# The second layer's feed-forward tiles 8 to 21, computed by seven products over both token chunks at once instead of over the two halves of each chunk

## The chip, the cores and the metric

The kernel runs on one core of one Trainium2 chip. The core has five engines that run their own instruction lists and meet by semaphores: TensorE (PE, matrix products; PEld is its weight load), VectorE (DVE), ScalarE (ACT), GpSimd (POOL) and SyncE (SP), which here only starts DMAs. The metric is the device time of one execution in microseconds, as the median of three runs.

## The reference, cut to what matters

A trunk of two residual layers works on 1024 tokens of 1024 channels, everything in float32. Layer 0 mixes tokens by a Conformer convolution, layer 1 by pooling over trailing windows; each layer then has a SwiGLU feed-forward part, and a norm ends the trunk.

```
for i in range(2):
    h = modulate(rms_norm(x, norm_mix_g[i]), sh_m, sc_m)
    y = conformer_conv(h, ...) if i == 0 else multiscale_pool(h, pool_w, pool_ls)
    x = x + (1 + g_m) * y
    h = modulate(rms_norm(x, norm_ffn_g[i]), sh_f, sc_f)
    y = (silu(h @ w_gate[i]) * (h @ w_up[i])) @ w_down[i]      # 1024 -> 2816 -> 1024
    x = x + (1 + g_f) * y
return rms_norm(x, final_g)
```

The change is in the feed-forward part of layer 1: its two products with `w_gate` and `w_up`, and what stands around them.

## The kernel before

**Tiling.** Channels lie on the 128 partitions, tokens along the free axis. The tokens are cut into two chunks of 512, A and B. `x[chunk][k]` is channel tile k (of 8) of a chunk and stays in SBUF. The hidden width 2816 is 22 tiles of 128, called tiles 0 to 21 below.

**Precision.** A float32 product is made of three fast ones: each operand is split into a high part `hi` (rounded to the fast type) and a low part `lo` (what the rounding left), and hi·hi, hi·lo and lo·hi are summed in PSUM. ACT makes `hi` by a copy, DVE makes `lo` by a subtraction. For many weights the `lo` is made without DVE: ACT writes minus `hi`, and a DMA started by POOL adds the weight from DRAM onto it.

**A plain tile** (`ffn_p1`) is 48 products of 512 columns: 8 input tiles × 3 for gate, the same for up. `ffn_p2` gives a tile pair's share of the down product: for each of the 8 output tiles d, six products and then one update of `x` by DVE (`update`, the rows `x<-dn,gains,x`). I call such a group of six a slot.

**Seven products instead of eight.** Most tiles run in pairs of hidden tiles (`Pair`, `ffn_pair`). The weight of a pair is seen as 2×2 blocks (two hidden tiles × two halves of the input channels), the input as 2×2 blocks (two halves of the channels × the two halves of 256 tokens in a chunk), and Winograd's form of Strassen's scheme gives the four result blocks by seven block products. A block product (`quad`) is 4 input tiles × 3 = 12 products of 256 columns. The scheme needs four sums of input blocks, made once for a chunk (`combined`: the tiles `thi`, `tlo`), and four sums of weight blocks, made for each pair and each chunk (`Pair.prepare`: `shi`, `slo`, `w`). A pair is two units (gate, then up), each of 84 products of 256 columns. Between its block products stand up to four slots of the down product of the pair before (`Downs.slot`).

**Order of work in layer 1, before.** Chunk A: tiles 0 and 1 plain, 2 to 17 in pairs, 18 to 21 plain, with the pooling mixer of B among the last; then B: tiles 0 and 1 plain, 2 to 21 in pairs, and `ending`, which makes the last down product in two halves of 256 columns and the final norm. `pooled` starts a chunk's mixer, then takes its output product (`pool_out`, the rows `y`), then the norm ahead of the feed-forward part (`norm`, the tiles `hhi`, `hlo`).

**What sets the order.** PE's list is the order in which the code is written. DVE, ACT, POOL and SP lists are set by a scheduler when the program is built, by priorities and its own estimate of when a thing is ready; every engine then takes its own list strictly in order. Background work is written as generators (`Task`), which `pace` and `finish` advance; `finish` and `need` write all that is left of a task at that place.

**Buffers that matter.** PSUM has eight banks: six named `mm` (`bank`) and two named `ca` (`spare_bank`). `output(name, True)` takes three from the six, then one from the two, so slots of the down product go round all eight. Weight tiles `w` have 9 buffers, raw weights `raw` 4, per-chunk tiles for `hhi`/`hlo` 16 each.

Of the kernel before, what the change touches and what calls it, by code (L numbers as in the profile page):

```python
# [16 lines left out]
P = 128  # L17
D = 1024
# [101 lines left out]
def trunk(ctx, tc, xT, c, vec, ada, adan, w1, w2, wgu, wdn, wpl, wph, out):  # L120
# [46 lines left out]
    raws = ctx.enter_context(tc.tile_pool(name="raws", bufs=RAW_BUFS))  # L167
    tmp = ctx.enter_context(tc.tile_pool(name="tmp", bufs=2))
    ps = ctx.enter_context(tc.tile_pool(name="ps", bufs=BANKS, space=bass.MemoryType.PSUM))

    uid = [0]

# [76 lines left out]
    def slot(ch, name, dt=F32R):  # L249

        return slots.tile([P, ch.n], dt, tag=f"s{ch.i}", name=nm(name))
# [37 lines left out]
        return t[:, :n]  # L289


    cact = cst.tile([P, D], F32, name="cact")
# [237 lines left out]
    def sum_sq(srcs, n, into=None):  # L530
        acc = None
        for s in srcs:
            if acc is None:
                acc = temp(n, "acc", 2) if into is None else into[:, :n]
                S_.activation(acc, s, AF.Square)
            else:
                sq = temp(n)
                S_.activation(sq, s, AF.Square)
                V_.tensor_tensor(acc, acc, sq, op=ADD)
            yield  # L540
        return acc
# [27 lines left out]
        if lows is not None:  # L569
            lows.append(V_.last.ins.name)  # L570

    def norm(ch, l, ffn, key, keep=False, squares=None, **kw):
# [7 lines left out]
        for k in range(KT):  # L580
            modulated(ch, l, ffn, h, rstd, k, lows if kw else None)
            yield

# [14 lines left out]
    def own(unit_):  # L598
        return unit_[0], tuple(Own(w) for w in unit_[1])
# [465 lines left out]
    FRONT, BACK = slice(0, QUAD), slice(QUAD, D)  # L1065
    f32 = lambda t: t.bitcast(F32)

    def combined(ch):

        other = chunks[1 - ch.i]  # L1070
        h = st["h", ch.i]
        got = st["T", ch.i] = []
        for k in range(KT // 2):
            whole = []
            for hi, lo in (h[k], h[k + KT // 2]):
                t = window(ch.n, "hf")
                V_.tensor_tensor(t, f32(hi), f32(lo), op=ADD)
                whole.append(t)
            a, b = whole
            q12, q34 = temp(ch.n, "tf"), temp(ch.n, "tf")  # L1080
            V_.tensor_tensor(q12[:, LEFT], a[:, LEFT], a[:, RIGHT], op=SUB)
            V_.scalar_tensor_tensor(q12[:, RIGHT], q12[:, LEFT], -1.0, b[:, RIGHT], op0=MUL, op1=SUB)
            V_.tensor_tensor(q34[:, LEFT], b[:, RIGHT], a[:, RIGHT], op=SUB)
            V_.scalar_tensor_tensor(q34[:, RIGHT], q12[:, RIGHT], -1.0, b[:, LEFT], op0=MUL, op1=SUB)
            if k == KT // 2 - 2:
                st["rows", ch.i] = V_.last.ins.name
            yield
            row = []
            for q in (q12, q34):
                hi, lo = slot(other, "thi"), slot(other, "tlo")  # L1090
# [208 lines left out]
    def ffn_mixed(ch, l, plain, until, at_end=False, beside=None):  # L1299
# [26 lines left out]
        if until == NF:  # L1326
# [4 lines left out]
        if not at_end:  # L1331
            for i in (4, -1):
                rest[i] = own(rest[i])
        return before, paired, rest

    def ending(ch, l, fs):

# [59 lines left out]
        return emit, tuple(wdn[l, f] for f in fs)  # L1397

    def final(ch):
        acc = yield from sum_sq(x[ch.i], ch.n, cact)  # L1400
# [266 lines left out]
        need(("T", ch.i))  # L1667
        add(us)

    before, pairs, rest = ffn_mixed(B, 0, PLAIN[0], UNTIL[0])  # L1670
    put(("T", 1), lambda: combined(B))
    add(before[:2])
    put(("stats", 0), lambda: pool_stats(A))
# [71 lines left out]
```

## Time and profile before

| | |
|---|---|
| three runs | 1793.75, 1795.19 and 1796.05 us; median 1795.19 |
| the profiled execution | span 1797.1 us from the first to the last instruction |
| PE busy | 1770.1 us, 98% of the span |
| DVE busy | 1402.7 us, 78% |
| ACT busy | 1042.8 us, 58% |
| POOL busy | 556.3 us, 31% |
| DMA | 321.85 MB, mean 179 GB/s |

The profile was taken on one execution of its own; only its span is known, and it is 1.9 us longer than the median of the runs. A stretch of the span is named by its start and end in us from the first instruction. An engine's instructions overlap a little, so the time from one start to the next is shorter than the duration of one. The lists of before and of the changed kernel are the same on PE up to the first paired block of chunk A in layer 1, which stands at 1093.6 us of the profiled span.

### The profile page before, as it was taken

Reading aid. Unit: us, or ns where it says so; the run is one execution under the profiler, and the core shown is the slowest. Engines: PE = TensorE matmul, PEld = TensorE weight load, DVE = VectorE, ACT = ScalarE, POOL = GpSimd, SP = SyncE. Lnnn points to the kernel's source line nnn. Section 1 sums busy time; section 2 is a strip of 40 time slices with the busy share of each in tenths; the row PEclk is TensorE's granted clock in tenths of the full one; section 3 lists DMA queues with packets and bytes.
Section 4 is the critical chain, followed back from the end, with each engine's and each line's share of the span. In section 5 each row is a group of like instructions: output and inputs, shape, how many; then the busy total and the mean of one; then the engine's idle time right before and its main releaser. Section 6 shows DMA issues by size and latency. Waiting matters only on the chain.

```text
span 1797.1 us, 27345 instructions
## 1 busy us (share of the span) xinstructions
PE 1770.1 (98%) x10178; PEld 1537.1 (86%) x10178; DVE 1402.7 (78%) x2270; ACT 1042.8 (58%) x1682; POOL 556.3 (31%) x604
## 2 busy tenths in 40 slices
PE   9999999999999999999999999999999999999997
PEld 7777777888888888899999889999998889999997
DVE  8688946898775328989996999878769998887865
ACT  4766665877646455555556356655554566555553
POOL 0388822987734121211113611101115111011112
PEclk9999999999999999999999999999999999999999
DMA  9968766897988988877765566455555765655442
GB/s 306 284 177 249 184 154 175 216 239 205 235 206 207 236 218 196 227 205 203 205 197 138 140 171 153 130 137 141 136 130 140 170 154 140 183 141 137 128 113 59
DMA packets 112921, 321.85 MB, mean 179 GB/s; under 512 B 11026, under 2 KB 21394, under 8 KB 112787
## 3 DMA queue, kind: packets, MB, share of 16 engines
q1 hardware_dynamic: 77936, 222.56, 37.5%
q0 software_dynamic: 33696, 96.48, 30.3%
q8 instruction: 80, 1.31, 0.3%
q10 hardware_dynamic: 1154, 1.05, 0.2%
q14 instruction: 55, 0.44, 0.1%
HBM read 315.85 MB, written 4.19 MB: 178 GB/s over the span
## 4 chain that ended last, share of the span: by engine, by line
PE 90%; DVE 3%; issue 2%; ACT 2%; DMA 2%; POOL 1%; ACTq 0%; DVEq 0%; SPq 0%; POOLq 0%
PE dn L137 25%; PE up L137 24%; PE gate L137 24%; PE y L137 5%; PE a L137 3%; PE g L137 2%; PE first L137 2%; ACT w L114 1%; PE ada L137 1%; DVE t L114 1%; DVE hlo L114 1%; DMA adaw<-in_adan_dram 1%; PE var L137 1%; PE rstd L137 1%; DMA w<-in_wgu_dram 1%
## 5 line engine op out<-in xcount | busy, mean ns | idle before, releaser
L137 PE MATMUL dn<-ghi,w 128*128 128x512 f32 (+1 forms) x1440 | 474.1, 387 | 0.6 <-ACT t L114 0.6
L114 ACT CAST w<-raw 128x512 fp32r<-128x512 f32 (+1 forms) x410 | 320.5, 784 | 169.6 <-PE up L137 73.5
L114 DVE SCALAR_TENSOR_TENSOR x<-dn,gains,x 128x512 f32<-128x512 f32 (+1 forms) x360 | 262.6, 736 | 66.4 <-PE dn L137 57.5
L137 PEld LDWEIGHTS dn<-ghi,w 128*128 128x128 f32 x1440 | 269.3, 189 | 50.7 <-ACT t L114 1.0
L114 ACT ACTIVATE w<-raw 128x1024 fp32r<-128x1024 f32 (+1 forms) x234 | 204.8, 875 | 165.5 <-PE dn L137 43.7
L1161 POOL DMA_DIRECT2D w<-in_wgu_dram x100 | 87.1, 873 | 633.9 <-PE up L137 203.2
L137 PE MATMUL dn<-glo,w 128*128 128x512 f32 (+1 forms) x720 | 279.3, 388 | 0.1
L137 PE MATMUL gate<-hhi,w 128*128 128x512 f32 (+1 forms) x1008 | 275.3, 348 | 0.9 <-ACT hhi L114 0.6
L137 PE MATMUL up<-hhi,w 128*128 128x512 f32 (+1 forms) x1008 | 275.0, 347 | 0.0
L114 POOL TENSOR_TENSOR pa<-pa,pr 128x512 f32<-128x512 f32 x176 | 251.3, 1565 | 18.3 <-ACT pr L114 15.5
L137 PEld LDWEIGHTS gate<-hhi,w 128*128 128x128 f32 x1008 | 179.7, 189 | 26.7 <-ACT hhi L114 0.7
L137 PEld LDWEIGHTS up<-hhi,w 128*128 128x128 f32 x1008 | 179.9, 189 | 24.5
L137 PE MATMUL gate<-hlo,w 128*128 128x512 f32 (+1 forms) x504 | 175.4, 348 | 1.5 <-DVE hlo L114 1.5
L137 PE MATMUL up<-hlo,w 128*128 128x512 f32 (+1 forms) x504 | 175.0, 347 | 0.0
L114 DVE SCALAR_TENSOR_TENSOR ca<-u,vecs,ca 128x512 f32<-128x512 f32 x244 | 170.6, 749 | 1.0
L114 DVE TENSOR_TENSOR w<-raw,w 128x512 fp32r<-128x512 f32 (+1 forms) x176 | 137.8, 789 | 32.1 <-ACT w L114 27.7
L137 PEld LDWEIGHTS dn<-glo,w 128*128 128x128 f32 x720 | 136.1, 189 | 20.4 <-POOL glo L114 0.6
L445 POOL DMA_DIRECT2D w<-in_wgu_dram x70 | 63.1, 906 | 244.8 <-ACT w L114 222.1
L114 ACT ACTIVATE pr<-u,vecs 128x512 f32<-128x512 f32 x176 | 119.9, 718 | 27.5 <-POOL pa L114 19.7
L114 ACT CAST shi<-ny 128x512 fp32r<-128x512 f32 x100 | 62.1, 621 | 119.9 <-PE gate L137 59.5
L114 DVE TENSOR_TENSOR t<-t,up 128x256 f32<-128x256 f32 (+1 forms) x86 | 52.3, 609 | 89.2 <-PE up L137 88.3
L137 PEld LDWEIGHTS gate<-hlo,w 128*128 128x128 f32 x504 | 95.3, 189 | 15.4 <-DVE hlo L114 2.6
(203 smaller groups left out, 3751.3 us busy)
## 6 DMA issues: line engine op xcount, KB each, us to landing
raw<-in_wgu_dram SPq DMA_DIRECT2D x176, 512.0 KB, 4.8
raw<-in_wdn_dram SPq DMA_DIRECT2D x88, 512.0 KB, 5.3
w<-in_wgu_dram POOLq DMA_DIRECT2D x70, 512.0 KB, 8.0
adaw<-in_ada_dram SPq DMA_DIRECT2D x64, 512.0 KB, 5.3
w<-in_wgu_dram POOLq DMA_DIRECT2D x100, 256.0 KB, 5.7
raw<-in_w_dram SPq DMA_DIRECT2D x42, 512.0 KB, 6.7
adaw<-in_adan_dram SPq DMA_DIRECT2D x32, 512.0 KB, 5.7
w<-in_w_dram POOLq DMA_DIRECT2D x32, 512.0 KB, 8.1
```

What stands on the lines that cost most here:

```text
L114: self.last = self.order(getattr(self.eng, name)(out, *args, **kw))
L137: last_mm[0] = nc.tensor.matmul(out, lhsT, rhs, start=start, stop=stop, **kw).ins.name
L445: order(nc.gpsimd.dma_start(as_src(lo), src, accum_op=ADD))
L1161: order(nc.gpsimd.dma_start(lo, src, accum_op=ADD))
```

## The change

The gate and up products of tiles 8 to 21 take the seven-product scheme over both chunks together: the two column blocks of the input are now chunk A and chunk B, 512 columns each, instead of the two halves of one chunk. A unit (`joint_unit`) is 84 products of 512 columns and serves both chunks; the weight sums are made once for both.

- Chunk A's tiles 0 to 7 run plain. Chunk B's pooling mixer and its norm run among them, so that both chunks' inputs are there before tile 8.
- The sums of input blocks are made by `joint_rows` after B's norm: for each of four steps k, five wide sums and their splits. The sums are named t1, t2, t3 and t4. There is not room for all: t1 and t4 and the first half of B's own input (`front`) are written to DRAM (`keep`), and t1 and t4 are read back in every unit into the same eight SBUF tiles (`streamed`), t4 after the product with t1, t1 after the product with t4.
- The low parts of the weight blocks are all made by DVE (`Joint.halves`) in place of the adding DMAs.
- The down products (`JointDowns`) have a slot for each output tile and each chunk, and take their banks from `spare_bank`. They stand at fixed places within the units (`GATE_SLOTS`, `UP_SLOTS`); the first unit takes all eight slots of A's tiles 6 and 7 in one piece, the second has none.
- After the joint units B alone takes its tiles 0 and 1 plain and 2 to 7 in pairs of 256 columns; sixteen slots of the last joint pair stand between tiles 0 and 1. The ending is as before, on tiles 6 and 7.

```diff
-PLAIN = (4, 2, 2)
-UNTIL = (18, 18, 22)
+PLAIN, UNTIL = 4, 18
+WHOLE = 8
+GATE_SLOTS = (6, 9, 12, 14, 17, 19, 22, 24)
+UP_SLOTS = (3, 6, 9, 11, 14, 17, 20, 23)
...
+    class JointDowns(Downs):
+        def __init__(self, l, fs, dps, chs):
+            super().__init__(None, l, fs, dps)
+            self.todo = [(d, ch) for d in self.todo for ch in chs]
+        def slot(self, out=None):
+            d, ch = self.todo.pop(0)
+            self.load(d // 2)
+            wt = self.tiles[d // 2]
+            b = (out or spare_bank)("dn")
...
+            update(ch, d, b, gate_f, self.l)
...
+    def joint_rows():
...
+        def split(q, tiles):
+            S_.copy(tiles[0], q)
+            V_.tensor_tensor(tiles[1], q, f32(tiles[0]), op=SUB)
+            return tiles
+        def keep(name, k, tiles):
+            for dst, t in zip(st["kept", name][k], tiles):
+                sync.dma_start(dst, f32(t))
+        def whole(h, t):
+            V_.tensor_tensor(t, f32(h[0]), f32(h[1]), op=ADD)
+            return t
+        for k in range(half):
+            keep("front", k, hb[k])
+            a, c, d = whole(ha[k], ...), whole(hb[k], ...), whole(hb[k + half], ...)
+            V_.tensor_tensor(a, a, c, op=SUB)
+            V_.tensor_tensor(c, d, c, op=SUB)
+            V_.scalar_tensor_tensor(d, a, -1.0, d, op0=MUL, op1=SUB)
+            st["t2"].append(split(d, ...))
+            b = whole(ha[k + half], temp(512))
+            V_.scalar_tensor_tensor(b, d, -1.0, b, op0=MUL, op1=SUB)
+            st["t1"].append(split(a, [slot(B, n) for n in ("t1hi", "t1lo")]))
+            keep("t1", k, st["t1"][k])
+            st["t3"].append(split(c, ...))
+            keep("t4", k, split(b, [tmp.tile([P, TMPW], F32R, tag="acc", name=nm("t4"), bufs=2) for _ in range(2)]))
...
+    def joint_unit(l, me, following, downs, later, first=False, last=False):
...
+            block(a, "w11", ha[:half], True)
+            S_.copy(ra, a)
+            block(left, "w12", ha[half:], True)
+            V_.tensor_tensor(ra, ra, left, op=ADD)
+            if first:
+                for each in downs:
+                    while each.todo:
+                        each.slot(lambda n: output(n, True))
+                finish(T["rows"])
+            block(a, "s2", st["t2"], False)
+            S_.copy(rb, a)
+            block(right, "s1", st.pop("t1"), True)
+            S_.copy(qb, right)
+            t4 = streamed("t4", B)
...
+            block(a, "s3", st["t3"], False)
+            V_.tensor_tensor(qb, qb, a, op=ADD)
+            block(right, "s4", hb[half:], False)
+            V_.tensor_tensor(rb, rb, right, op=ADD)
+            block(a, "w22", t4, False)
...
+                st["t1"] = streamed("t1", B)
...
-    before, pairs, rest_a = ffn_mixed(A, 1, PLAIN[1], UNTIL[1], False, (("stats", 1), lambda: pool_stats(B, cact)))
-    add(before[:1])
-    put_eager(("T", 0), lambda: combined(A))
-    add(rest[-1:] + before[1:])
-    paired(A, pairs)
-    need(("stats", 1))
-    pooled(rest_a[:-1], B, OUT_AT)
-    before, pairs, rest = ffn_mixed(B, 1, PLAIN[2], UNTIL[2], True, ("final_a", lambda: final(A)))
+    us, joint_pend = [], rest[-1]
+    for f in range(0, WHOLE, 2):
+        us += [ffn_p1(A, 1, f, True), joint_pend, ffn_p1(A, 1, f + 1, True)]
+        joint_pend = ffn_p2(A, 1, [f, f + 1], True)
...
+    need(("nf", 1))
+    put_eager("rows", joint_rows)
+    joint, last = ffn_joint(1, WHOLE)
+    add(joint)
+    before, pairs, rest = ffn_mixed(B, 1, 2, WHOLE, True, ("final_a", lambda: final(A)))
     add(before[:1])
-    put_eager(("T", 1), lambda: combined(B))
-    add(rest_a[-1:] + before[1:])
+    put_eager(("T", 1), lambda: combined(B, (A, A, B, B)))
+    add(last)
+    add(before[1:])
     paired(B, pairs)
     add(rest)
```

The built programs show where this puts instructions. The first place is DVE's list just ahead of the first unit's products with sums of input blocks. Before, for chunk A's first pair (`tlo` is the low part of a sum of input blocks, `slo` that of a sum of weight blocks, `acc` and `ny` are sums of weight blocks):

```order
L114 SCALAR_TENSOR_TENSOR x_7_92<-dn_10223,gains,x_7_92 128x512
L114 TENSOR_TENSOR w_10411<-raw_10330,w_10411 128x512
L114 TENSOR_TENSOR ny_10363<-ny_10351,raw_10241 128x512
L114 TENSOR_TENSOR slo_10354<-ny_10351,shi_10353 128x512
L114 TENSOR_TENSOR acc_10422<-raw_10332 128x512
L114 TENSOR_TENSOR slo_10360<-acc_10357,shi_10359 128x512
L114 SCALAR_TENSOR_TENSOR tf_10286<-tf_10285,hf_10283 128x256
L114 TENSOR_TENSOR tlo_10304<-tf_10285,thi_10303 128x512
```

Now, the rows of the last two of four steps of `joint_rows` (`ha`, `hb` are sums of a chunk's high and low parts; `t2lo_11501` and `t2lo_11535` are the low parts of t2 for steps k = 2 and 3):

```order
L117 TENSOR_TENSOR t2lo_11501<-hb_11495,t2hi_11500 128x512
L117 TENSOR_TENSOR t_2225_11518<-t_11504,t_2224_11517 128x512
L117 TENSOR_TENSOR ha_11525<-ha_11525,hb_11527 128x512
L117 TENSOR_TENSOR hb_11529<-hhi_10997,hlo_10998 128x512
L117 TENSOR_TENSOR hb_11527<-hb_11529,hb_11527 128x512
L117 TENSOR_TENSOR t1lo_11542<-ha_11525,t1hi_11541 128x512
L117 SCALAR_TENSOR_TENSOR hb_11529<-ha_11525,hb_11529 128x512
L117 TENSOR_TENSOR t3lo_11548<-hb_11527,t3hi_11547 128x512
L117 SCALAR_TENSOR_TENSOR t_11538<-hb_11529,t_11538 128x512
L117 TENSOR_TENSOR t2lo_11535<-hb_11529,t2hi_11534 128x512
```

Where four sums of input blocks of a chunk stood among the weight work, five sums of 512 columns for both chunks and their low parts now stand in a row, twelve rows of DVE for each k; in DVE's list the last low part of t2 is the 74th row from the update `x_7` after the slots of A's tiles 4 and 5 on, that update counted (21 SCALAR_TENSOR_TENSOR and 53 TENSOR_TENSOR, all of 512 columns).

The second place is DVE's list beside the slots that stand alone ahead of B's pairs. Before, in the like place ahead of A's pairs, between the updates for the first slots:

```order
L114 SCALAR_TENSOR_TENSOR x_0_85<-dn_10149,gains,x_0_85 128x512
L114 SCALAR_TENSOR_TENSOR tf_10235<-tf_10235,hf_10233 128x256
L114 TENSOR_TENSOR tf_10236<-hf_10233,hf_10231 128x256
L114 TENSOR_TENSOR tlo_10212<-tf_10170,thi_10211 128x512
L114 SCALAR_TENSOR_TENSOR x_1_86<-dn_10157,gains,x_1_86 128x512
L114 TENSOR_TENSOR glo_10111<-t_10112,ghi_10110 128x512
L114 SCALAR_TENSOR_TENSOR tf_10236<-tf_10235,hf_10233 128x256
L114 TENSOR_TENSOR w_10334<-raw_10241,w_10334 128x512
L114 SCALAR_TENSOR_TENSOR x_2_87<-dn_10175,gains,x_2_87 128x512
```

Now, from the update for the second of the sixteen slots to that for the third:

```order
L117 SCALAR_TENSOR_TENSOR x_0_87<-dn_14880,gains,x_0_87 128x512
L117 SCALAR_TENSOR_TENSOR tf_14990<-tf_14990,hf_14988 128x256
L117 TENSOR_TENSOR tf_14991<-hf_14988,hf_14986 128x256
L117 TENSOR_TENSOR glo_14841<-t_14842,ghi_14840 128x512
L117 TENSOR_TENSOR tf_15064<-hf_15060 128x256
L117 SCALAR_TENSOR_TENSOR tf_14991<-tf_14990,hf_14988 128x256
L117 TENSOR_TENSOR w_15125<-raw_14847,w_15125 128x512
L117 TENSOR_TENSOR acc_15136<-raw_14849 128x512
L117 TENSOR_TENSOR acc_15148<-raw_14847,raw_14849 128x512
L117 TENSOR_TENSOR hf_15062<-hhi_10997,hlo_10998 128x512
L117 TENSOR_TENSOR tlo_15029<-tf_14990,thi_15028 128x512
L117 SCALAR_TENSOR_TENSOR x_1_80<-dn_14888,gains,x_1_80 128x512
```

Ten rows stand there between two updates, and the slots have two banks instead of eight. From the first to the last of the sixteen updates are 44 rows: 16 updates, 21 others of 512 columns and 7 of 256. The third place is SP's list within a joint unit. Before, the paired stage had weight loads alone:

```order
L1182 DMA raw_10696<-in_wdn_dram 128x2x512
L1108 DMA raw_10802<-in_wgu_dram 128x1024
L1108 DMA raw_10804<-in_wgu_dram 128x1024
L1182 DMA raw_10891<-in_wdn_dram 128x2x512
L1108 DMA raw_10982<-in_wgu_dram 128x1024
```

Now loads of t4 stand around a weight load (`t_2141` and its neighbours are t4 in DRAM):

```order
L1189 DMA raw_12124<-in_wdn_dram 128x2x512
L150 DMA t_2376_12221<-t_2141_11260 128x512
L150 DMA t_2377_12222<-t_2142_11261 128x512
L150 DMA t_2378_12225<-t_2143_11262 128x512
L150 DMA t_2379_12226<-t_2144_11263 128x512
L1115 DMA raw_12266<-in_wgu_dram 128x1024
L150 DMA t_2380_12229<-t_2145_11264 128x512
L150 DMA t_2381_12230<-t_2146_11265 128x512
```

A unit's two weights, its share of the down weights, eight tiles of t4 and eight of t1 now go through that one list, each behind the one above it.

More of the change, by code (lines that the diff above doesn't have):

```diff
@@ L579, in norm @@
         lows = []
-        for k in range(KT):
+        for k in ks:
             modulated(ch, l, ffn, h, rstd, k, lows if kw else None)
@@ new lines, in trunk @@
+    class JointDowns(Downs):
[7 more added lines that the diff above has]
+            b = (out or spare_bank)("dn")
+            for i, f in enumerate(self.fs):
+                g = st["g", ch.i, f]
+                for j, (wp, a) in enumerate(((0, 0), (0, 1), (1, 0))):
+                    matmul(b, wt[:, wp, i, (d % 2) * P : (d % 2 + 1) * P], g[a], start=i + j == 0, stop=i == 1 and j == 2)
+            update(ch, d, b, gate_f, self.l)
+            if d % 2 == 0:
+                self.load(d // 2 + 1)
+            pace()
@@ new lines, in ffn_joint, with begin @@
+    def ffn_joint(l, start):
+        mates = [Joint(l, f, which) for f in range(start, NF, 2) for which in range(2)]
+        mine = [[JointDowns(l, (start - 2, start - 1), dps, (A,)) for dps in ((0, 1), (2, 3))], []]
+        for f in range(start, NF, 2):
+            mine += [[JointDowns(l, (f, f + 1), dps, (A, B))] for dps in ((0, 1), (2, 3))]
+        def begin(take):
+            mates[0].front()
+            for each in mine[0]:
+                for dp in each.dps:
+                    each.load(dp)
+        us = [(begin, ())]
+        for i, me in enumerate(mates):
+            later = mine[i + 1]
+            us.append(joint_unit(l, me, mates[i + 1] if i + 1 < len(mates) else None, mine[i], later[0] if later else None,
+                                 i == 0, i + 1 == len(mates)))
+        return us, [alone(d) for d in (mine[-2][0], mine[-1][0])]
@@ L1668, in paired @@
         add(us)
-    before, pairs, rest = ffn_mixed(B, 0, PLAIN[0], UNTIL[0])
+    before, pairs, rest = ffn_mixed(B, 0, PLAIN, UNTIL)
     put(("T", 1), lambda: combined(B))
```

160 lines of the change are left out of this document (150 added, 10 removed).

## The prediction

> **What bounds the kernel now.** I read the page from the top: busy time, then the chain that ended last, then windows over layer 1's paired stage.
>
> ```profile
> span 1797.1 us, 27345 instructions
> PE 1770.1 (98%) x10178; PEld 1537.1 (86%) x10178; DVE 1402.7 (78%) x2270; ACT 1042.8 (58%) x1682; POOL 556.3 (31%) x604
> PE 90%; DVE 3%; issue 2%; ACT 2%; DMA 2%; POOL 1%; ACTq 0%; DVEq 0%; SPq 0%; POOLq 0%
> core 0: us, PE busy (x) PEld busy (x) DVE busy (x) ACT busy (x) POOL busy (x), PEclk, DMA share, GB/s
> 1100.00:1340.00 240.00, 240.00 (x1674) 224.27 (x1673) 187.85 (x309) 134.84 (x256) 27.23 (x38) 1.00 0.55 142
> 1400.00:1456.00 56.00, 55.32 (x252) 45.40 (x251) 51.18 (x96) 30.74 (x48) 7.82 (x9) 1.00 0.66 152
> 1460.00:1760.00 300.00, 299.59 (x2097) 279.99 (x2096) 239.29 (x392) 166.55 (x321) 32.81 (x38) 1.00 0.54 140
> ```
>
> Within A's pairs (1100 to 1340) PE is busy in every microsecond at full clock (PEclk 1.00), and B's pairs are nearly the same. There, time falls only if PE has fewer or cheaper products, and rises by every wait that is new on PE. The start of B's pairs (1400 to 1456) leaves PE idle for 0.68 us. So the sum has two kinds of terms: what the columns cost, and new waits in PE's list.
>
> **The change part by part. Products.** The chain in order of time shows whole blocks of gate products (start, length, count):
>
> ```profile
> 1003.44 5.44 PE gate L137 x24
> 1119.35 2.86 PE gate L137 x24
> ```
>
> 24 products of 512 columns take 5.44 us, 226.7 ns each; 24 of 256 columns take 2.86 us, 119 ns each. Two of the small cost 238 ns, 11 more than one of the large. PE's list loses 2520 products of 256 columns (4200 become 1680) and gains 1272 of 512; the down products are the same in number. −2520 × 0.1190 = −299.9 us and +1272 × 0.2267 = +288.4 us: **−11.5 us**.
>
> The Trainium skill ("TensorE: Matmul & The Clock Gate", section "Back-to-back issue gap") gives an isolated product N/2.4 + 2.5 ns, 109.2 for 256 columns and 215.8 for 512. By that the exchange would gain 0.7 us and the sum would be 10.8 us higher; the rows differ from it for both sizes, by more for the small one, and they decide.
>
> **The wait for the rows of the joint input.** In the first joint unit PE's list has, after the slots of A's tiles 4 and 5: tile 7's 48 products (10.9 us by the row above), two blocks of 12 (5.4), the eight slots of tiles 6 and 7 (48 products, 10.9), and then the product with t2, of which nine products (2.0) can go before the fourth k is needed. That is 29.2 us of work. On DVE, 74 rows stand from the update `x_7` after the slots of tiles 4 and 5 to t2's fourth low part. Their pace is read where DVE works without a pause:
>
> ```profile
> 1446.81 0.69 DVE L114 TENSOR_TENSOR ny<-acc,raw 128x512 f32<-128x512 f32 x1
> 1447.40 0.69 DVE L114 TENSOR_TENSOR slo<-acc,shi 128x512 fp32r<-128x512 f32 x1
> 1448.01 0.75 DVE L114 SCALAR_TENSOR_TENSOR x<-dn,gains,x 128x512 f32<-128x512 f32 x1
> 1448.67 0.42 DVE L114 TENSOR_TENSOR tf<-hf,hf 128x256 f32<-128x256 f32 x1
> 1449.00 0.42 DVE L114 SCALAR_TENSOR_TENSOR tf<-tf,hf 128x256 f32<-128x256 f32 x1
> ```
>
> From start to start a TENSOR_TENSOR of 512 columns takes 0.59 to 0.61 (I use 0.60), a SCALAR_TENSOR_TENSOR 0.66, and rows of 256 columns 0.33 and 0.34. So 21 × 0.66 + 53 × 0.60 = 45.7 us after `x_7` begins, which cannot begin before PE has made slot 7. The difference, 16.5 us, is idle time on PE even if DVE arrives on time. It does not: from B's norm (`rstd`) on, DVE has 22 rows (19 SCALAR_TENSOR_TENSOR, 3 others) ahead of `x_7`, behind an ACT copy:
>
> ```profile
> L114 ACT COPY ny<-rstd 128x512 f32<-128x512 f32 x4 | 2.3, 580 | 18.3 <-PE rstd L137 18.3
> ```
>
> 0.58 + 19 × 0.66 + 3 × 0.60 = 14.9 us, while PE goes through the eight slots of tiles 4 and 5 in 10.9: DVE is 4.0 us late. **+20.5 us** (16.5 if DVE arrives on time; 24 if an ACT copy that DVE's subtraction needs comes late in some of the steps). Behind these rows on DVE stand the updates of tiles 6 and 7's slots; they only hold PSUM banks, eight of them for eight slots, so they add nothing of their own.
>
> **The clock after that wait.** PE stands for over 15 us. The nearest row is the first norm, where PE waits for DVE too:
>
> ```profile
> 72.00:78.00 6.00, 4.55 (x24) 3.58 (x23) 4.03 (x9) 6.00 (x9) 3.27 (x3) 0.98 1.05 257
> 78.00:84.00 6.00, 6.00 (x25) 5.00 (x24) 1.68 (x10) 4.49 (x7) 6.00 (x7) 0.74 1.06 270
> ```
>
> After 1.45 us of missing work the granted clock over the next 6 us is 0.74: 6 × 0.26 = 1.6 us lost. **+1.6** (0 to 3.2, if it happens at both new waits). The skill's clock gate (the same page, "Part 1: The HAM clock gate") says that an idle window sends PE to half rate and that about 3.4 us of work bring it back, an estimate of 1.7 us for one long wait; the 0.74 agrees.
>
> **The sixteen slots that stand alone.** They follow each other on PE with nothing between them, from two banks, so slot n waits for the update of slot n−2. DVE has 16 updates, 21 other rows of 512 columns and 7 of 256 in that stretch: 16 × 0.66 + 21 × 0.60 + 7 × 0.335 = 25.5 us against 16 × 1.36 = 21.8 of products. That DVE lags there is seen in before's like place, hidden by eight banks:
>
> ```profile
> 1434.62 10.88 PE dn L137 x48
> 1436.69 0.75 DVE L114 SCALAR_TENSOR_TENSOR x<-dn,gains,x 128x512 f32<-128x512 f32 x1
> 1449.34 0.75 DVE L114 SCALAR_TENSOR_TENSOR x<-dn,gains,x 128x512 f32<-128x512 f32 x1
> ```
>
> Eight slots took PE 10.88 us; their first and last updates start 12.65 us apart. With two banks PE follows this pace: the stretch takes at least 1.5 us (to the first update) + 25.5 = 27.0, +5.2, and DVE's list arrives about 3 us late, since rows on a gate weight of the next plain tile, whose buffer PE frees only there, stand among the updates. **+8** (5, on time, to 11, twice as late).
>
> **t1, t4 and weights from DRAM.** Eight tiles of 256 KB each replace t1 by t4 and back, 2.1 MB a time. The rates seen:
>
> ```profile
> 20.00:60.00 40.00, 40.00 (x179) 33.11 (x178) 35.97 (x51) 19.81 (x31) 0.00 (x0) 1.00 0.97 327
> raw<-in_wgu_dram SPq DMA_DIRECT2D x176, 512.0 KB, 4.8
> x<-in_xT_dram SPq DMA_DIRECT2D x16, 256.0 KB, 5.9
> ```
>
> At 327 GB/s 2.1 MB take 6.4 us, the last tile about 6.4 + 3 after the first is freed (a 512 KB load alone lands in 4.8, of which 1.6 is its bytes). Between the first freed tile of t1 and the first use of t4 PE has eleven steps of three products, 11 × 0.68 = 7.5 us, and the last use is three steps (2.0) later: 9.4 against 9.5 in the units without slots, and five slots more (14.3 us) in the others. PE's list hides it, barely in the first two units. **+1** (0 to +8, a late tile in both bare units and small ones elsewhere). The low parts that DVE now makes in place of POOL's adding DMAs lie under PE: a pair of units has 34.8 us of DVE rows at the pace above against 59.8 us of PE (168 + 96 products of 226.7 ns). Without that cover each would cost its 0.60 us. The writes of t1, t4 and front go into the stretch of the first wait, whose length DVE sets.
>
> **What goes.** The waits at the old paired starts, 0.68 us at B's by the 1400 row and little at A's: **−1** (0 to −2); B's pairs still start once.
>
> **Sum** against the profiled span: 1797.1 − 11.5 + 20.5 + 1.6 + 8 + 1 − 1 = 1815.7. The profiled execution's span is 1.9 us over the median of the runs, so **1814 us** by that measure, +1.0%. The low bounds give −11.5 + 16.5 + 0 + 5 + 0 − 2 = +8.0 (1803), the high ones −11.5 + 24 + 3.2 + 11 + 8 + 0 = +34.7 (1830).
>
> **Rivals.** *DVE is no obstacle (faster).* If rows of joint_rows, which read and write SBUF alone, ran twice as fast at 512 columns as I price them, 45.7 us would be about 24 (0.33 × 74), under the 29.2 us of cover, and the alone slots would be paced by PE: 1795 − 11.5 − 1 + 1 = 1783. It decides from 0.39 us a row down. Against it: `ny<-acc,raw` and `slo<-acc,shi` above are such rows and take 0.60. *The streams set the pace (slower).* If a DMA of t1 or t4, issued behind weight loads in SP's one list, is on average 3 us late in 13 of 14 units, +40: 1855. It decides once 2.1 MB need over 14 us with the landing, under 190 GB/s. For it: DMA share is already 0.55 at 142 GB/s in A's pairs. Against it: 327 GB/s were moved in 20:60, with loads of whole rows, and a unit asks for 4.2 MB + 1 MB of gate or up weights + some 1 MB of down weights in 29.9 us, about 210 GB/s. *No gain by columns.* If a 512 column product in the scheme costs two small ones, 238 ns, the products come to +2.8 instead of −11.5: 1828. Against it: the row of 5.44 us; for it, only that no row of before has blocks of twelve at this width. *Half clock in the alone slots.* If many short waits lower the clock as a long one does, 16 slots at half rate take 43.6 us instead of 29.8 (21.8 + 8): +14, 1828. Against it: 72:78 has 1.45 us idle at 0.98.
>
> The skill's same page (section "A second HAM failure mode: psum-queue depth-cycling") says that waits between groups of products, as PSUM banks go round, can swing the clock; this is that last case, and no row of before shows slots that wait for banks.
>
> **How the numbers follow.** Chances: the sum 0.78; DVE no obstacle 0.08; the streams 0.10; no gain by columns 0.02; half clock 0.02. About 0.2%, 3.6 us, is what a measurement of this kernel can tell from no change. The sum's own bounds (1803 to 1830) lie beyond that, and I leave 0.02 of its 0.78 to "same", for bounds that all fall low. Faster 0.08, same 0.02, slower 0.90. The range 1801 to 1832 holds the sum with both 1828 cases; outside it are 1783, 1855 and a few hundredths of the sum, together just under 0.2.
>
> **What would show it.** Columns: blocks of 24 gate products at 5.44 us in the joint units, a bare unit at 84 × 0.2267 = 19.0 us and one with eight slots at 29.9. First wait: some 20 us of PE idle ahead of and within the first product with t2, released by DVE or ACT on t2's tiles, and PEclk under 1 behind it. Alone slots: short waits of `dn` products for DVE's update, 8 us in all over 16 slots, and nothing like it in joint units. Streams: waits of gate or up products released by a DMA, under 1 us in units with slots. The forecast is wrong if DVE has pauses in the stretch of the 74 rows, so that something else is late, if the slots do not wait for updates, or if a stream's wait comes back in every unit.

## The result and the profile after

The changed kernel takes 1817.14 us (median of four runs, 1816.68 to 1817.62) against 1795.26 (1793.75 to 1796.05): the ratio is 1.0121, interval 1.0107 to 1.0136, so it is slower by 21.9 us. (The kernel before has one run more here than ahead of the prediction.) The forecast was 1814, the range 1801 to 1832.

From the page of the changed kernel:

```profile
PE 1765.0 (97%) x8930; PEld 1477.8 (81%) x8930; DVE 1315.9 (72%) x2107; ACT 940.4 (52%) x1439; POOL 513.9 (28%) x550
```

PE is busy for 5 us less, and the span, 1815.2 us, is 18.1 us longer. Part of that comparison is chance: the lists are the same up to the first paired block, and that block starts at 1093.43 us in the profiled execution of before and at 1090.51 in this one. From there on the windows of the two kernels read (span of the window, PE, PEld, DVE, ACT, POOL busy with counts, PEclk, DMA share, GB/s; before first):

```profile
1093.43:1797.00 703.57, 692.10 (x4555) 634.19 (x4553) 566.51 (x943) 384.12 (x716) 108.23 (x124) 1.00 0.54 137
```

```profile
1090.51:1815.00 724.49, 689.21 (x3307) 577.21 (x3305) 495.93 (x815) 282.11 (x480) 63.18 (x63) 0.98 0.57 176
```

So the changed part costs 20.9 us: 1248 products fewer, and PE idle for 35.3 us instead of 11.5. The waits of PE in that stretch say where:

```profile
PE gate L140 <- ACT t2hi L117: 10.0, 3, 3.6
PE dn L140 <- DVE x L117: 8.7, 5, 3.3
PE gate L140 <- DVE t2lo L117: 3.8, 3, 1.9
PE rstd L140 <- DVE col L117: 2.9, 2, 1.5
PE dn L140 <- POOL glo L117: 2.9, 1, 2.9
```

Before had the 2.9 at `rstd`, waits of 0.6 and 0.3, and no other that is named. What is new stands in two places. The first is the stretch of `joint_rows`, the second the sixteen slots that stand alone; between them lie the joint units:

```profile
1200.00:1250.00 50.00, 33.39 (x119) 24.62 (x118) 47.11 (x78) 18.27 (x33) 4.52 (x1) 0.80 0.45 155
1250.00:1640.00 390.00, 389.82 (x1717) 321.82 (x1716) 236.92 (x358) 125.80 (x213) 3.51 (x4) 1.00 0.61 207
1645.00:1685.00 40.00, 31.29 (x118) 23.63 (x117) 31.56 (x55) 11.63 (x20) 2.62 (x3) 0.91 0.29 78
```

At 226.7 ns, 119 products are 27.0 us of 50 and 118 are 26.8 of 40: 23.0 us are lost in the first place and 13.2 in the second. In between 1717 products take 390 us, 227 ns each, with 0.18 us idle.

How the first wait ends, on PE and on DVE:

```profile
1228.53 0.51 PE L140 MATMUL gate<-t2hi,w 128*128 128x512 f32 x1 [3.64 <-ACT t2hi L117]
1235.27 0.80 PE L140 MATMUL gate<-t2hi,w 128*128 128x512 f32 x1 [3.16 <-ACT t2hi L117]
1242.02 0.80 PE L140 MATMUL gate<-t2hi,w 128*128 128x512 f32 x1 [3.16 <-ACT t2hi L117]
```

```profile
1196.82 0.75 DVE L117 SCALAR_TENSOR_TENSOR x<-dn,gains,x 128x512 f32<-128x512 f32 x1
...
1242.44 0.69 DVE L117 TENSOR_TENSOR t2lo<-hb,t2hi 128x512 fp32r<-128x512 f32 x1
```

ACT is named for the longest waits, but it only copies what DVE has just summed, one k every 6.75 us (eleven rows; the twelfth, the sum of A's high and low part that t4 needs, was made earlier). From the update `x_7` (1196.82) to the end of the last low part (1243.13) DVE needs 46.3 us and stands still for 0.6 of it.

The second place, PE and then DVE:

```profile
1646.37 2.88 PE L140 MATMUL dn<-gpair,w 128*128 128x512 f32 x12
1652.55 4.61 PE L140 MATMUL dn<-gpair,w 128*128 128x512 f32 x12 [3.30 <-DVE x L117]
1659.52 4.56 PE L140 MATMUL dn<-gpair,w 128*128 128x512 f32 x12 [2.35 <-DVE x L117]
```

```profile
1651.75 0.75 DVE L117 SCALAR_TENSOR_TENSOR x<-dn,gains,x 128x512 f32<-128x512 f32 x1
...
1653.01 0.75 DVE L117 SCALAR_TENSOR_TENSOR x<-dn,gains,x 128x512 f32<-128x512 f32 x1
...
1658.62 0.75 DVE L117 SCALAR_TENSOR_TENSOR x<-dn,gains,x 128x512 f32<-128x512 f32 x1
```

The first slot is done by 1647.7 (its six products start at 1646.37); its update starts at 1651.75. Between the second update and the third lie the ten rows that the order shows, 5.6 us, and with two banks PE waits for each such clump.

### The profile page after: what moved, and what is told of

Same layout as the page of the kernel before. It is cut to its first block, busy times and chain, and to the rows that moved or that the text cites. A ratio compares the mean times of both kernels' runs of the same rounds, so it can differ in the third digit from the quotient of the medians.

```text
span 1815.2 us, 24581 instructions
## 1 busy us (share of the span) xinstructions
PE 1765.0 (97%) x8930; PEld 1477.8 (81%) x8930; DVE 1315.9 (72%) x2107; ACT 940.4 (52%) x1439; POOL 513.9 (28%) x550
## 5 line engine op out<-in xcount | busy, mean ns | idle before, releaser
L117 ACT CAST w<-raw 128x512 fp32r<-128x512 f32 (+1 forms) x338 | 276.5, 822 | 185.5 <-PE dn L140 55.8
L140 PE MATMUL dn<-ghi,w 128*128 128x512 f32 (+1 forms) x992 | 316.6, 386 | 1.4 <-DMA w<-in_wdn_dram 0.8
L140 PE MATMUL gate<-hhi,w 128*128 128x512 f32 (+1 forms) x928 | 284.1, 374 | 0.6 <-ACT hhi L117 0.6
L140 PE MATMUL up<-hhi,w 128*128 128x512 f32 (+1 forms) x928 | 284.5, 374 | 0.0
L117 ACT ACTIVATE w<-raw 128x1024 fp32r<-128x1024 f32 (+1 forms) x182 | 175.5, 964 | 198.0 <-PE up L140 63.5
L452 POOL DMA_DIRECT2D w<-in_wgu_dram x76 | 68.4, 904 | 650.9 <-ACT w L117 641.4
L140 PEld LDWEIGHTS dn<-ghi,w 128*128 128x128 f32 x992 | 185.3, 189 | 37.0 <-DMA w<-in_wdn_dram 1.2
L140 PEld LDWEIGHTS gate<-hhi,w 128*128 128x128 f32 x928 | 171.0, 188 | 32.9 <-ACT hhi L117 0.7
L140 PEld LDWEIGHTS up<-hhi,w 128*128 128x128 f32 x928 | 171.0, 188 | 31.0
L140 PE MATMUL dn<-glo,w 128*128 128x512 f32 (+1 forms) x496 | 191.2, 385 | 3.0 <-POOL glo L117 2.9
L140 PE MATMUL dn<-gpair,w 128*128 128x512 f32 x672 | 173.4, 396 | 8.8 <-DVE x L117 8.7
L140 PE MATMUL gate<-hlo,w 128*128 128x512 f32 (+1 forms) x464 | 173.5, 374 | 0.3 <-DVE hlo L117 0.3
L140 PE MATMUL up<-hlo,w 128*128 128x512 f32 (+1 forms) x464 | 173.3, 374 | 0.0
L140 PEld LDWEIGHTS dn<-gpair,w 128*128 128x128 f32 x672 | 127.8, 191 | 38.8 <-DVE x L117 6.5
L117 ACT ACTIVATE pr<-u,vecs 128x512 f32<-128x512 f32 x176 | 120.2, 717 | 29.2 <-POOL pa L117 21.5
L117 DVE TENSOR_TENSOR t<-t,up 128x512 f32<-128x512 f32 (+1 forms) x79 | 51.4, 652 | 108.4 <-PE up L140 107.5
L1168 POOL DMA_DIRECT2D w<-in_wgu_dram x40 | 34.9, 879 | 266.5 <-ACT w L117 81.0
L140 PEld LDWEIGHTS dn<-glo,w 128*128 128x128 f32 x496 | 93.9, 189 | 19.5 <-POOL glo L117 3.9
```

Source lines behind the costliest of these rows:

```text
L117: self.last = self.order(getattr(self.eng, name)(out, *args, **kw))
L140: last_mm[0] = nc.tensor.matmul(out, lhsT, rhs, start=start, stop=stop, **kw).ins.name
L452: order(nc.gpsimd.dma_start(as_src(lo), src, accum_op=ADD))
L1168: order(nc.gpsimd.dma_start(lo, src, accum_op=ADD))
```

## The experiments

All of them are edits of the changed kernel. Times are medians; where a difference to the changed kernel is given, it is to 1817.14. Ratios in brackets are to the kernel before, which was timed again beside each group of runs; its median there lay between 1794.27 and 1796.11. So a difference of up to some 2 us between two runs is not told from none.

**eight_banks.** The sixteen slots go round all eight banks.

```diff
-    def alone(downs):
+    def alone(downs, *wide_out):
...
-                downs.slot()
+                downs.slot(*wide_out)
...
-        return us, [alone(d) for d in (mine[-2][0], mine[-1][0])]
+        return us, [alone(d, lambda n: output(n, True)) for d in (mine[-2][0], mine[-1][0])]
```

> The sixteen slots that stand alone take their banks from all eight, not from two. Theory (two banks make PE follow DVE's updates one by one, and the short stops halve the clock twice): in the trace of the changed kernel this stretch holds 14.1 us over its products; with eight banks the first eight slots run without a stop and the ninth needs an update that DVE has made long before. 11 to 14 us go: 1803 to 1806 us against 1817.1. Rival (DVE's total sets the stretch, 25.5 us of rows and a start some 3 us late against 21.8 us of products, however many banks): only the clumping goes, 5 us: 1812. Rival (what follows the slots waits instead, for a weight tile whose rows stand among the updates): 1817.

1802.68 us, 14.5 less (1.0039 of before, 1.0025 to 1.0053). The window over the slots now reads

```profile
1640.00:1670.00 30.00, 30.00 (x134) 24.86 (x133) 28.23 (x52) 12.66 (x23) 2.62 (x3) 1.00 0.43 115
```

```profile
1644.53 21.92 PE L140 MATMUL dn<-gpair,w 128*128 128x512 f32 x96
```

PE has no idle time and full clock, with DVE as busy as 28.2 of 30 us: the sixteen slots take 21.8 us. DVE still ends its last update at 1672.2, 5.9 us after PE has gone on, so its total and its late start do not set the stretch. The first theory holds, a little past its upper end. But the run changed more than the banks. DVE's list came out in another order, with 38 rows instead of 44 from the first to the last update, and three instead of ten between the second and the third:

```profile
1651.48 0.74 DVE L117 SCALAR_TENSOR_TENSOR x<-dn,gains,x 128x512 f32<-128x512 f32 x1
...
1653.42 0.74 DVE L117 SCALAR_TENSOR_TENSOR x<-dn,gains,x 128x512 f32<-128x512 f32 x1
```

The share of the order was not measured. As an estimate from the changed kernel's own rows: with eight banks the 13th slot could start at 1662.7 (1646.37 + 12 × 1.36), and it needs the fifth update, which began at 1664.22 and ended at 1665.0. With a like stop at the 14th some 3 us would stay, so most of the 14.5 us is the banks' part.

**no_sums.** DVE's part of the first wait.

```diff
-            a, c, d = whole(ha[k], ...), whole(hb[k], ...), whole(hb[k + half], ...)
+            a, c, d = window(512, "ha"), window(512, "hb"), window(512, "hb")
+            a0, c0, d0 = f32(ha[k][0]), f32(hb[k][0]), f32(hb[k + half][0])
...
-            V_.tensor_tensor(a, a, c, op=SUB)
+            V_.tensor_tensor(a, a0, c0, op=SUB)
```

> The sums of the joint input are made from the high parts alone: the sixteen additions of a high to a low part (four for each k) are left out, so the result is less exact. It takes 16 x 0.60 = 9.6 us of DVE's rows out of the stretch ahead of the first product with t2. Theory (DVE's rows set that wait, 16.6 us of idle PE in three steps and the slots): PE's idle time falls by 9 to 10 us and some half clock with it: 1806 to 1808. Rival (ACT's copies of t2's high part set it: 10.0 of the 13.8 us there are put down to ACT): each step still waits for its copy, less than 3 us go: 1814 to 1817.

1807.76 us (1.0068, 1.0051 to 1.0084), 9.4 less for 16 rows of 0.60 (9.6). The waits put down to ACT's copies fall with DVE's rows, which the rival forbids:

```profile
PE gate L140 <- ACT t2hi L117: 4.0, 2, 2.7
...
PE gate L140 <- DVE t2lo L117: 1.6, 2, 1.3
```

On DVE the way from `x_7` to the end of the last low part of t2 has 58 rows instead of 74 and takes 36.8 us instead of 46.3:

```profile
1195.52 0.74 DVE L117 SCALAR_TENSOR_TENSOR x<-dn,gains,x 128x512 f32<-128x512 f32 x1
...
1231.63 0.68 DVE L117 TENSOR_TENSOR t2lo<-hb,t2hi 128x512 fp32r<-128x512 f32 x1
```

So DVE's rows set the first wait, microsecond for microsecond as far as the scatter of the runs (1805.96 to 1808.87) tells.

**ten_plain.** `WHOLE = 10`.

> Ten plain tiles of chunk A instead of eight, and the joint units start at tile 10. B's mixer output and norm keep their distance from the first joint unit, so they move back with it. Theory (only the work between B's norm and the first product with t2 covers DVE's rows): the wait stays, and the columns cost 96 x 0.2267 + 168 x 0.1190 - 168 x 0.2267 = +3.7 us: 1820 to 1822. Rival (the stage as a whole has too little time for DVE, and any two more plain tiles give it more): the wait falls by up to 20 us: 1801 to 1805.

1821.53 us (1.0144, 1.0129 to 1.0160), 4.4 more, where the theory said 3.7. The wait is there again, 34 us later, with 9.6 and 3.8 us at t2. More plain tiles cover nothing when B's norm moves back with them.

**glo_dve.** The edit asked for tile 7's low part on DVE, where it was already; no instruction changed.

> The low part of tile 7's hidden values (glo) is made by DVE instead of POOL, whose one row took 4.52 us there and let PE stand 2.86 us ahead of the slots, with half clock behind it. Theory (DVE's chain from the update x_7 to t2's last low part sets when the first unit goes on; a stop ahead of it only moves there): 0 to +1 us, 1816 to 1819, and the time of the stop comes back at t2. Rival (the stop adds to the wait): 2.9 us and about 2 of half clock go, 1812 to 1813.

1817.87 us. It tells nothing of POOL's row, only how well a median repeated here: within 0.7 us, with single runs from 1815.40 to 1819.21.

**glo_tile6.** The same for tile 6, whose row it was.

```diff
-        us += [ffn_p1(A, 1, f, True), joint_pend, ffn_p1(A, 1, f + 1, True)]
+        us += [ffn_p1(A, 1, f, True, f + 2 == WHOLE), joint_pend, ffn_p1(A, 1, f + 1, True)]
```

> The row of 4.52 us on POOL was the low part of tile 6's hidden values, not of tile 7's, which DVE had made already: the run glo_dve changed no instruction. This one gives tile 6's to DVE. Theory (DVE's chain to t2's last low part sets when the first unit goes on, and a stop of PE ahead of it costs nothing of its own): the stop of 2.86 us ahead of the slots is gone, PE comes earlier to t2 and waits there for longer: 1816 to 1819. Rival (the stop adds to the wait): 1812 to 1813.

1817.93 us (1.0132, 1.0118 to 1.0145): 0.8 more, no difference that can be told, and not the 4 to 5 us less of the rival. The stop for POOL is gone. The waits at t2 are longer by 2.4 us, and 1.3 us now go to `glo` rows of DVE:

```profile
PE gate L140 <- ACT t2hi L117: 12.8, 3, 6.4
...
PE gate L140 <- DVE t2lo L117: 3.4, 3, 1.6
```

So a stop ahead of a longer one cost nothing of its own that these runs can tell.

**streams_twice.** Each load of t1 and t4 twice.

```diff
-                sync.dma_start(f32(t), src)
+                for _ in range(2 if name != "front" else 1):
+                    sync.dma_start(f32(t), src)
```

> Each load of t1 and t4 is issued twice (4.2 MB a time instead of 2.1), the second with the same data. Theory (the streams lie far under PE's work, as no wait of the joint units is put down to them): at 327 GB/s the doubled load takes 12.8 us and some 3 of landing against 14.3 to 16.3 of work in a unit with slots; a unit without slots is late by 5 to 6 us, the others by 0 to 2: 1820 to 1840. Rival of the prediction (the streams are near their limit already): each doubled load is late by its whole 6.4 us in every unit, twice a unit: 1900 or more.

1862.86 us (1.0382, 1.0363 to 1.0400), 45.7 more: neither number. The steady units of both kernels, the changed one first:

```profile
1300.00:1600.00 300.00, 300.00 (x1325) 248.40 (x1324) 186.66 (x281) 92.17 (x160) 0.00 (x0) 1.00 0.55 193
```

```profile
1300.00:1600.00 300.00, 294.93 (x1276) 239.37 (x1275) 177.66 (x265) 87.92 (x153) 0.00 (x0) 0.99 0.90 314
```

At 193 GB/s the streams cost nothing; at 314 they cost 49 products, 11 us, in 300. Over the whole run 22.8 us of PE's waits are now put down to these loads. Another part lies in the first two units, which have no slots to cover the loads:

```profile
1250.00:1300.00 50.00, 40.50 (x144) 29.26 (x143) 21.60 (x34) 13.48 (x24) 0.00 (x0) 0.86 0.97 345
```

144 products are 32.6 us of 50. Most of the rest lies at the end of the joint units, where loads of `front` come on top: from 1640 to 1680 PE has 109 products, 24.7 us of 40, and 9.7 us of waits for t. The cover holds the streams as they are, but not twice the bytes, and least of all where no slots stand.

**rows_early.** B's output and norm one unit earlier, `joint_rows` behind tile 6.

```diff
+        if i == len(us) - 3:
+            need(("nf", 1))
+            unit(lambda take: st.__setitem__(("h", 1), st["hn", 1]))
+            put_eager("rows", joint_rows)
...
-        if i == len(us) - 4:
+        if i == len(us) - 5:
```

> B's mixer output and norm stand one unit earlier (behind the slots of A's tiles 2 and 3, not behind tile 5), and joint_rows starts behind tile 6 instead of behind tile 7; nothing else is moved. The same rows on DVE now have tile 7 and eight more slots ahead of the first product with t2 as cover. Counted as in the prediction, the row that is late by most now leaves DVE 3.9 us late instead of 19.4. Theory (the wait is DVE's rows less the work between B's norm and t2): 14 to 19 us go, 1798 to 1803 against 1817.1. Rival (the wait moves: the output product y, now at 1147 us, comes before the last rows of B's mixer, which end on POOL at 1145): PE stops there for 5 to 10 us and half of the gain is gone: 1806 to 1812.

1814.23 us (1.0114, 1.0098 to 1.0129): 2.9 less by the medians, but the interval lies over that of the changed kernel (1.0107 to 1.0136), so a gain is not shown. Neither theory had the place of the loss. Its longest wait, and those at t2:

```profile
PE dn L140 <- ACT ghi L117: 6.8, 1, 6.8
...
PE gate L140 <- ACT t2hi L117: 2.7, 1, 2.7
...
PE gate L140 <- DVE t2lo L117: 0.8, 1, 0.8
```

At t2 3.5 us are left of 13.8, as the count of rows had it (3.9). But the norm's rows now come on DVE ahead of tile 5's own product, which starts at 1188.22:

```profile
1186.90 1.41 DVE L117 SCALAR_TENSOR_TENSOR hlo<-t,mod,hhi 128x512 fp32r<-128x512 f32 x2
1188.22 0.68 DVE L117 TENSOR_TENSOR t<-t,up 128x512 f32<-128x512 f32 x1
```

PE has reached the slots of tiles 4 and 5 at 1182.0 and stands there for tile 5's `ghi`:

```profile
1189.62 0.80 PE L140 MATMUL dn<-ghi,w 128*128 128x512 f32 x1 [6.75 <-ACT ghi L117]
```

The rows on DVE are in a strict order, and what I moved forward pushed back what PE needs first.

**both.** rows_early with eight_banks.

> rows_early and eight_banks together. Theory (the two waits are independent): 1817.1 - 14.4 (measured by eight_banks) - 14 to 19 = 1784 to 1789, under the 1795 to 1796 of the kernel before by 0.4 to 0.7%; what is left is the columns' gain of 11 to 14 us less some 4 us of wait. Rival (a gain in the one stage is lost in the other, or in B's last pairs): 1795 or more.

1800.02 us (1.0037, 1.0024 to 1.0049). The sum of the two measured differences is 1817.1 − 14.5 − 2.9 = 1799.7, so within some 2 us the two places do not act on each other. Only the share of rows_early was overrated: to eight_banks alone (1.0039) it adds nothing that can be told.

**ten_early.** `WHOLE = 10`, eight banks, B's output and norm where the changed kernel has them (behind tile 5), `joint_rows` behind tile 8.

```diff
-WHOLE = 8
+WHOLE = 10
...
-        if i == len(us) - 4:
+        if i == len(us) - 7:
```

> Ten plain tiles as in ten_plain, but B's mixer output and norm stay where the changed kernel has them (behind tile 5), so they get no nearer to the slots of tiles 4 and 5 than there; joint_rows starts behind tile 8, and the alone slots have eight banks. In rows_early the gain at t2 (15 us) was lost again in the slots of tiles 4 and 5, whose ghi came 6.8 us late because the norm's rows had moved ahead of tile 5's own rows on DVE. Theory (cover between the norm and t2 counts, if no other wait is made): the row that is late by most leaves DVE 2.7 us late, some 5 to 7 us of waits stay of 23.4, the columns cost 3.7, the eight banks bring 14.4: 1817.1 - 14.4 + 3.7 - 17 = 1787 to 1792, under the kernel before by 0.2 to 0.5%. Rival (the rows of DVE in this stage are too many wherever they stand, and the stop only moves again): 1800 or more, like rows_early with eight banks.

1801.16 us (1.0033, 1.0020 to 1.0046): the rival's side. t2 is down to 2.6 us, and a new stop stands ahead of it:

```profile
PE dn L140 <- POOL glo L117: 4.8, 1, 4.8
PE gate L140 <- ACT t2hi L117: 1.8, 1, 1.8
...
PE gate L140 <- DVE t2lo L117: 0.8, 1, 0.8
```

DVE itself stood for 7.3 us earlier in this stretch, at a row on a weight that was not yet loaded, with the rows of the joint input behind it:

```profile
1216.20 0.69 DVE L117 TENSOR_TENSOR ny<-raw,raw 128x512 f32<-128x512 f32 x1 [7.30 <-DMA raw<-in_wgu_dram]
```

**ten_early_glo** gave tile 8's low part to DVE.

> ten_early with the low part of tile 8's hidden values made by DVE instead of POOL. In glo_tile6 this brought nothing, since PE then waited at t2 for longer. Theory (a stop ahead of a longer wait is free, but counts once that wait is short): where ten_early's stop of some 3 us for POOL's row is still there, 1 to 3 us go against ten_early. Rival (DVE is late at t2 by its own rows, one more makes it later): 0 to +1 us against ten_early.

1799.43 us (1.0021, 1.0012 to 1.0029). POOL's 4.8 us are still there; the row is tile 9's. The 1.7 us to ten_early is within the two intervals: inconclusive.

**ten_early_all_glo** gave those of tiles 6 to 9 to DVE, and the scheduler a higher priority for the tiles' own rows from tile 5 on. The two were not run apart.

> ten_early with the low parts of the hidden values of tiles 6 to 9 all made by DVE. In ten_early_glo the long row of POOL was still there (4.8 us of waiting put down to POOL's glo): it was tile 9's. Theory (POOL's row is slow only because DVE works without a pause beside it, and with t2's wait down to 2.6 us a stop ahead of it counts): 4.8 us and some 2 of half clock behind it go, against up to four more rows on DVE (2.4 us): 1793 to 1797, no slower than the kernel before. Rival (DVE is the limit of the stage, and its rows come back at t2): 1800 to 1802.

1798.08 us (1.0018, 1.0008 to 1.0028), the lowest median of all, though not told from ten_early_glo, and still not under before. POOL is gone from the waits; 3.1 us of the 4.8 now are DVE's:

```profile
PE dn L141 <- DVE glo L118: 3.1, 1, 3.1
```

**both_gate_first** is both, with tile 5's rows ahead of the norm's and the low parts of tiles 4 to 7 on DVE.

```diff
-                    if k % 4 == 3:
+                    if k % 4 == 3 and not ((l, ch.i, f, k) == (1, 0, 5, KT - 1) and o is outs[1]):
                         pace()
             gated(ch, f, outs, soon)
+            if (l, ch.i, f) == (1, 0, 5):
+                pace()
```

> both (eight plain tiles, output and norm of B one unit earlier, eight banks) with tile 5's own rows on DVE put ahead of the norm's, and the low parts of tiles 4 to 7 made by DVE. Theory (both lost 11.4 us in the slots of tiles 4 and 5 to rows that were only in the wrong order): that stop goes; by the order of rows t2's last low part leaves DVE 12.6 us late instead of 3.4 since weight rows of the joint units now stand among the rows, so about 15 us of waits stay of 20: 1793 to 1798. Rival (the order costs nothing by itself, DVE's total in the stage does): 1800 to 1803, the loss only back at t2.

1800.44 us (1.0024, 1.0014 to 1.0033): again the rival. The stop at tile 5 is gone, and 10 us are at the first unit's weights and at t2:

```profile
PE gate L141 <- ACT t2hi L118: 5.0, 1, 5.0
PE gate L141 <- DVE t2lo L118: 2.6, 2, 1.5
PE gate L141 <- ACT w L118: 2.4, 1, 2.4
```

Of the five arrangements that try to get rid of both waits none is faster than before, and each interval lies above 1; all keep 7 to 16 us of idle time in this one stage by their lists of waits. That DVE's total is too large there is not shown, since in ten_early it also stood idle; whether an order of its rows exists that hides them all stays open.

## Why the prediction was right, and where it was off

The direction, the time (3 us low) and both places were right. Term by term:

- **Products, −11.5.** The prices hold: 227 ns in the joint units and 119 in the pairs of 256 columns that are left. "No gain by columns" falls.
- **The wait for the rows, +20.5, and the clock, +1.6.** Together 22.1 foreseen, 23.0 measured. DVE's 45.7 us for 74 rows were 46.3. no_sums shows that the rows are the cause. Counted as in the prediction, PE ends the slots of tiles 4 and 5 at 1192.08, where tile 7 begins, and takes t2's fourth k at 1242.02. That is 49.9 us for 29.2 of work, a wait of 20.7. In the window from 1200 to 1250 only 16.6 us are idle time (2.9, 10.0 and 3.8); the other 6.4 are mostly products at half clock, since the wait comes in pieces with single products between them. These are tile 7's first product, and a window at the end of the wait with a granted clock of 0.50:

  ```profile
  1192.08 0.39 PE L140 MATMUL gate<-hhi,w 128*128 128x512 f32 x1
  ```

  ```profile
  1230.00:1246.00 16.00, 6.86 (x13) 3.82 (x14) 14.44 (x24) 6.07 (x10) 0.00 (x0) 0.50 0.43 164
  ```

  The term held because DVE sets when the wait ends, whatever PE does meanwhile. The stop for POOL's `glo` was not foreseen and was free for the same reason (glo_tile6).
- **The slots that stand alone, +8 (5 to 11).** This is the term that was mis-sized: 13.2 us, above its own upper bound, and 14.5 by eight_banks. The mechanism, two banks and DVE late, was right, and DVE's first update came 5.4 us after the slots began where I had 4.5. I priced what follows by DVE's sum of rows; but DVE itself stood in it for 4.6 us (for a late load, 1.36, and for PE, 0.47 to 0.94 five times), for the most part because PE and DVE take turns over two banks, and the clumps of rows make the stops long enough to halve the clock twice. My rival "half clock in the alone slots" had 0.02 and happened in part: about 4.5 of the 13.2 us lie beyond the 8.7 of idle time.
- **Streams, +1.** 0.2 us idle in 390. The rival's point, "under 190 GB/s", was not tested as such; streams_twice shows that 314 GB/s are to be had in these units and that the cover is used up before twice the bytes.
- **What goes, −1.** By difference 20.9 − 23.0 − 13.2 − 0.2 + 11.5 = −4.0. Of it 0.9 are waits of before (0.6 and 0.3). About 3 us more are a cost that the prediction left out: a slot that stands between products of 256 columns takes longer than one between products of 512. The chain in order of time, before first:

  ```profile
  1106.67 1.38 PE dn L137 x6
  ```

  ```profile
  1301.78 1.36 PE dn L140 x6
  ```

  From the first paired block on, 135 slots of before stand between products of 256 columns and take 1.391 us at the mean, against 1.364 in the joint units; in the changed kernel 19 are left. An estimate from that is 116 × 0.027 = 3.1 us.
- **The base.** The span of before was 1.9 us above the runs, that of after is 1.9 below them (1815.2 and 1817.1). Taking the sum as a difference to the median was right.

In sum +5.2 at the slots, +0.9 at the first wait, −0.8 for the streams and −3.0 for what goes turn the 18.6 of the forecast into the 20.9 of the windows. That the total missed by less than its worst term is in part luck, since two errors cancel.

"DVE is no obstacle" falls with no_sums: 9.4 us for sixteen rows.

## What to carry to other kernels

Cheaper products are worth what is left after the work that prepares them: a one-time set of vector rows ahead of a stage is hidden only by matrix work that stands between its last input and its first use, so count both before trading. Where matrix work drains through a vector engine, compare the number of PSUM banks with the longest run of other rows between two drains, not with the vector engine's total; and look at the order again after such a change, since it can come out another way. And a wait that is moved is gone only if nothing that was pushed back by the move is needed earlier.

## What the runs showed of the hardware

**Short stops halve the clock.** In the first of these windows PE had just stood 2.86 us for `glo`, in the second 3.30 us for an update; in the third a stop of 1.53 us, which ended at 1675.87, left the clock alone:

```profile
1212.00:1218.00 6.00, 6.00 (x21) 4.76 (x20) 6.00 (x11) 1.14 (x2) 0.00 (x0) 0.72 0.11 44
1651.00:1657.00 6.00, 4.45 (x12) 3.32 (x12) 6.00 (x13) 1.30 (x3) 0.00 (x0) 0.72 0.28 87
1675.00:1681.00 6.00, 5.10 (x21) 3.94 (x22) 5.00 (x9) 0.03 (x1) 0.00 (x0) 1.00 0.01 2
```

At the first norm, in the rows of the prediction, 1.45 us of missing work were followed by 0.74, so the length of a stop alone does not decide it.

**A GpSimd row can stretch beside a VectorE that does not pause.** The tile view of `glo` on POOL (min, median, max in ns):

```profile
L117 POOL TENSOR_TENSOR glo<-t,ghi x14: 1283/1311/4522, 366.8 to 1207.1; 128x512 fp32r<-128x512 f32 x14
```

The longest is the one at 1207.07, while DVE ran its rows back to back; it ended at 1211.59, and DVE had come to a halt ahead of 1211.62 to wait for it:

```profile
1211.62 0.69 DVE L117 TENSOR_TENSOR t<-hhi,hlo 128x512 f32<-128x512 f32 x1 [0.58 <-POOL glo L117]
```

DVE's own rows beside it kept their 0.69 us. The Trainium skill ("SBUF — State Buffer", section "SBUF: two separate sides") says that VectorE rows with two SBUF inputs and GpSimd share a pair of ports by an exclusive lock for a whole instruction, so that the later one is blocked. The trace agrees that one of the two loses time, here GpSimd alone; but one blocked turn would be some 0.7 us, and here it was 3.2 over the median. In rows_early two rows of VectorE stretched instead, to 2.89 us together, beside `glo` rows of GpSimd of 1.61 and 1.52 us:

```profile
1190.62 2.89 DVE L117 TENSOR_TENSOR t<-hhi,hlo 128x512 f32<-128x512 f32 x2
```

What decides which of them waits, no run here shows.
